# Heads' sums of squares by one fp32 matmul, held operands and another order in the mixer

## The chip, the cores and the metric

The kernel runs on one core of a Trainium2 chip. The metric is the device time of one execution in microseconds, as the median of several runs. Beside the times there is one profiled execution, with every instruction of the five engines: TensorE (PE, its weight loads PEld), VectorE (DVE), ScalarE (ACT), GpSimd (POOL) and SyncE (SP, which issues the DMAs).

## The reference

A decoder trunk of two layers over 512 positions of width 1024. Each layer adds half a SwiGLU feed-forward, a mixer, and half a second feed-forward, each on the RMS-normed stream. Layer 0 mixes by a gated linear recurrence, layer 1 by stick-breaking attention with 16 heads of 64, whose keys and values come from the stream after layer 0. Keys and queries are normed per head:

```python
def shared_kv(x, kv_gain, w_kv, k_gain):
    hkv = rms_norm(x, kv_gain)
    k, v = jnp.split(hkv @ w_kv, 2, axis=-1)
    k = rms_norm(heads(k), k_gain)
    return k, heads(v)

xc = causal_depthwise_conv(rec, conv_w, conv_b)          # rec, gate: h @ w_in
r = sigmoid(block_diag_linear(xc, w_r, b_r)); i = sigmoid(block_diag_linear(xc, w_i, b_i))
a = exp(-8 * r * softplus(-lam)); u = sqrt(1 - a * a) * i * xc
h_t = a_t * h_{t-1} + u_t;   out = (h * gelu(gate)) @ w_out
```

## The kernel before

Activations lie transposed, 128 features by 512 positions to a tile. Every product is made in three matmuls: operand and weight are each split in a high part of type fp32r (a cast) and a low part (what is left, also fp32r), and high x high, low x high and high x low are summed in PSUM. `Weights.split` (L81) does it for weights of 128x1024 (w_hi by ScalarE or GpSimd, w_lo by VectorE), three buffers of each going round. `mm` (L200) issues a matmul. Outside the blocks under `tc.manual_schedule`, a scheduler that works from priorities and modelled durations orders each engine's instructions; the engines then run them strictly in that order, with semaphores for what they need of each other.

The stages, by start in the trace: first feed-forward of layer 0 (0 us), its mixer (356), second feed-forward (519), keys and values (866), first feed-forward of layer 1 (971), attention with its queries (1313), second feed-forward (1528).

**The mixer** walks `RG_ORDER` (L44): "rec" m is a tile of the recurrent branch (24 matmuls), "gate" m one of the gate branch (24), "ri" b the two gates r and i of a block of two tiles (24 matmuls, on the split outputs xc of `conv` (L557) of tiles 2b and 2b+1). What follows a step is queued one to three steps later: conv after its rec, `lru_1` to `lru_3` after an ri, `gate_1` and `gate_2` after a gate. The numbers in the names w_hi102 and so on are places in the plan of weights, 102 being the eleventh entry of the order.

**Keys.** For each of eight pairs of heads there are 24 matmuls into k, then `head_norm` (L668): kx is k over the layer's norm (VectorE), t its square (ScalarE). For all keys and all queries but the first, GpSimd casts t to a high part and VectorE takes the low part (L675, L676), and two fp32r matmuls with `blk`, a block matrix of ones, sum the squares of each head into hs. For query 0 (`qt` given) one matmul takes t and blk as fp32 (L681). Then ScalarE makes y, the inverse root, in three passes, VectorE corrects and multiplies in three (L689 to L691), and the result is split (kh, kl) and stored to DRAM. `head_norm` is a generator in three parts; the caller runs a part of the pair before between the products.

**Values.** Two groups g of four psum tiles, four chunks c each, 24 matmuls to a chunk; hkv is the stationary operand. `v_out` splits and stores them.

**The next feed-forward's operands.** `normed` (L330) makes from two tiles of the stream the seven combinations of its quarter blocks that `pair` (L368) multiplies by seven sums of weight blocks (a form of 24 matmuls over 256 columns each): two multiplications by gain and norm (L335), four sums (L344) and three splits (low parts at L342, L346, L348), nine instructions on VectorE. They depend on the norm r3 alone and on x, so the scheduler may put them early. They are called in the values' loop at three places of g = 0 and one of g = 1 (L767). The first matmuls of the feed-forward need all four.

Of the kernel before, what the change touches and what calls it, by code (L numbers as in the profile page):

```python
# [7 lines left out]
F32 = mybir.dt.float32  # L8
# [32 lines left out]

RG_ORDER = [("rec", 0), ("rec", 1), ("rec", 2), ("rec", 3), ("ri", 0), ("gate", 0), ("ri", 1), ("rec", 4), ("rec", 5), ("gate", 1), ("ri", 2),  # L44
            ("rec", 6), ("rec", 7), ("gate", 2), ("gate", 3), ("ri", 3), ("gate", 4), ("gate", 5), ("gate", 6), ("gate", 7)]

# [101 lines left out]
def trunk(ctx, tc, a, out):  # L150
# [47 lines left out]
        cur.tp = open_pool("tp")  # L198

    def mm(o, l, r, start, stop):  # L200
        nc.tensor.matmul(o, l, r, start=start, stop=stop, skip_group_check=True)  # L201


    prm = cp.tile([P, NPRM], F32, name="prm")
# [122 lines left out]
        nc.vector.tensor_tensor(out=lo, in0=xt, in1=hi.bitcast(F32), op=ALU.subtract)  # L327
        return hi, lo

    def normed(j, g, r, name):  # L330

        e = cur.ep.tile([P, 8, HS], F32, tag="e", name=f"e{name}{j}")
        for k in range(2):
            xt = x[2 * j + k].rearrange("p (c t) -> p c t", c=2)
            nc.vector.scalar_tensor_tensor(out=e[:, 2 * k:2 * k + 2], in0=xt, scalar=gain(g, 2 * j + k), in1=r.rearrange("p (c t) -> p c t", c=2), op0=ALU.mult, op1=ALU.mult)  # L335
        hi = cur.ht.tile([P, 7, HS], F32R, tag="hh", name=f"hh{name}{j}")
        lo = cur.ht.tile([P, 7, HS], F32R, tag="hl", name=f"hl{name}{j}")
        b11, b12, b21, b22 = (e[:, k] for k in range(4))
# [329 lines left out]
    def head_norm(ps, r, g, name, dst, tags, qt=None):  # L668

        kx, t = temp("sq", "kx" + name), temp("acc", "t" + name)  # L670
        nc.vector.tensor_tensor(out=kx, in0=ps, in1=r, op=ALU.mult)
        nc.scalar.activation(out=t, in_=kx, func=AF.Square)
        if qt is None:
            hi, lo = (spare(*tags[j], n + name) for j, n in ((0, "th"), (1, "tl")))
            nc.gpsimd.tensor_scalar(out=hi, in0=t, scalar1=1.0, scalar2=0.0, op0=ALU.mult, op1=ALU.add)  # L675
            nc.vector.tensor_tensor(out=lo, in0=t, in1=hi.bitcast(F32), op=ALU.subtract)  # L676
        yield
        ss = psum("hs" + name)
        y = temp("y", "y" + name, bufs=1)
        if qt is not None:  # L680
            mm(ss, blk.bitcast(F32), t, True, True)  # L681
        else:
            mm(ss, blk, hi, True, False)
            mm(ss, blk, lo, False, True)
        nc.scalar.activation(out=y, in_=ss, func=AF.Ln, scale=1.0 / HD, bias=epsc)
        nc.scalar.activation(out=y, in_=y, func=AF.Exp, scale=-0.5)
        nc.scalar.activation(out=t, in_=y, func=AF.Square)
        yield
        nc.vector.scalar_tensor_tensor(out=t, in0=ss, scalar=HD * EPS, in1=t, op0=ALU.add, op1=ALU.mult)  # L689
        nc.vector.scalar_tensor_tensor(out=y, in0=t, scalar=-3.0 * HD, in1=y, op0=ALU.add, op1=ALU.mult)  # L690
        nc.vector.scalar_tensor_tensor(out=y, in0=kx, scalar=g, in1=y, op0=ALU.mult, op1=ALU.mult)  # L691
        if qt is not None:

            halves = [slice(e * HD, (e + 1) * HD) for e in range(2)]
            for e in range(2):
                nc.gpsimd.tensor_scalar(out=qt[halves[e], 0, e], in0=y[halves[e]], scalar1=1.0, scalar2=0.0, op0=ALU.mult, op1=ALU.add)
                nc.scalar.copy(out=qt[halves[1 - e], 0, e], in_=y[halves[e]])
            for e in range(2):
                for d in (e, 1 - e):
                    nc.vector.tensor_tensor(out=qt[halves[d], 1, e], in0=y[halves[e]], in1=qt[halves[e], 0, e].bitcast(F32), op=ALU.subtract)  # L700
            return
        hi, lo = (spare(*tags[j], n + name) for j, n in ((2, "kh"), (3, "kl")))
        nc.gpsimd.tensor_scalar(out=hi, in0=y, scalar1=1.0, scalar2=0.0, op0=ALU.mult, op1=ALU.add)
        nc.vector.tensor_tensor(out=lo, in0=y, in1=hi.bitcast(F32), op=ALU.subtract)
        for j, t in enumerate((hi, lo)):
            nc.sync.dma_start(dst[j], t.bitcast(F32))
# [7 lines left out]
    for p in range(NPAIR):  # L714
# [15 lines left out]
            nc.vector.scalar_tensor_tensor(out=rc, in0=rt, scalar=-3.0 * D, in1=rc, op0=ALU.add, op1=ALU.mult)  # L730
            nc.vector.tensor_scalar(out=rc, in0=rc, scalar1=-0.5 / D, scalar2=None, op0=ALU.mult)
        kd.append(dp.tile([2, P, S], F32, tag="kd", name=f"kd{p}"))
        gen = head_norm(ps, r3, kg, f"k{p}", kd[p], ((cur.tp, "t3"), (cur.tp, "t4"), (cur.tp, "rec"), (cur.tp, "rec")))
        run(gen)
        run(pend)
        pend = gen
# [12 lines left out]
    for g in range(2):  # L749
        pv = [psum(f"v{g}{s}") for s in range(NCH)]  # L750
        pvs.append(pv)
        if g == 1:
            close_pools(2)
            more_weights()
        for c in range(4):
            hi, lo = W.get(("v", g, c))
            for s in range(NCH):
                ss = slice(s * P, (s + 1) * P)
                for k in range(2):
                    xh, xl = hkv[2 * c + k]  # L760
                    ks = slice(k * S, (k + 1) * S)
                    mm(pv[s], xh[:, ss], hi[:, ks], c == 0 and k == 0, False)
                    mm(pv[s], xh[:, ss], lo[:, ks], False, False)
                    mm(pv[s], xl[:, ss], hi[:, ks], False, c == 3 and k == 1)
            if g == 0 and c < 2:
                run(pend)
            if g == 0 and c > 0 or g == 1 and c == 1:  # L767
                h3.append(normed(len(h3), G_FFN1[1], r3, "n3"))
            if g == 1 and c == 0:
                v_out(0, pvs[0])  # L770

# [136 lines left out]
    def query(p):  # L908

        ps = psum(f"q{p}")  # L910
        if p == 0:
            qts[p] = xp.tile([P, 2, 2, S], F32R, tag="x", name=f"qp{p}")
        return steps(ps, W.get(("q", p)), h4), lambda: head_norm(ps, r4, qg, f"q{p}", qd[p], ((cur.hp, "ch"),) * 4, qts.get(p))


    early = []
# [159 lines left out]
```

## Time and profile before

| | us |
|---|---|
| median of 3 runs (lowest to highest) | 1880.0 (1879.5 to 1881.9) |
| the profiled execution | 1879.0 |
| its span, first to last instruction | 1877.3 |
| keys and values, 865.7 to 970.9 | 105.2 |
| attention with its queries, 1312.9 to 1527.5 | 214.6 |

The span is counted from the first instruction; the profiled execution's own time is 1.7 us more. A row by time gives start, length, engine, line, operation, tiles and shapes, and in brackets the idle time ahead of it with what ended it. A row by line gives busy time and mean length in ns, then the idle time ahead of such instructions. Names stand without their numbers there (hsk is hs of any key pair). Ends of TensorE's rows are modelled; its starts are measured.

### The profile page before, as it was taken

The numbers are of one execution on the slowest core, as the hardware profiler recorded it, in microseconds if no ns is written. First come the engines' busy times: TensorE is split into PE (matmuls) and PEld (weight loads), VectorE is DVE, ScalarE is ACT, GpSimd is POOL, SyncE is SP. The second block draws the span as 40 slices with busy tenths as digits, with TensorE's granted clock in tenths as the row PEclk, the third lists the DMA queues.
The fourth block names the chain that finished last, engine by engine and source line by source line (L and its number), as shares of the span: only waits on it lengthen the run. The fifth ranks groups of instructions, "written<-read, shape, count | busy, mean of one in ns | idle before, by whom it ended". The sixth has DMA issues, their size and how long they took to land.

```text
span 1877.3 us, 27297 instructions
## 1 busy us (share of the span) xinstructions
PE 1839.0 (98%) x11040; PEld 1633.1 (87%) x11040; DVE 1382.4 (74%) x1709; ACT 921.7 (49%) x1282; POOL 156.6 (8%) x196
## 2 busy tenths in 40 slices
PE   9999999999999999999899999999898999999999
PEld 7889989778789899997689899898676789899897
DVE  8958657698788586576978667585799879667483
ACT  6525435368555254354545335254588745345251
POOL 1000000032000000000200000000365500000000
PEclk9999999999999999999999999999999999999999
DMA  6223423222415134232474324134365431425131
GB/s 225 91 79 98 139 71 98 79 79 82 154 46 179 46 101 124 90 93 76 135 213 126 111 79 146 56 111 148 117 188 154 147 92 46 146 79 157 57 109 61
DMA packets 73118, 207.87 MB, mean 111 GB/s; under 512 B 7584, under 2 KB 17056, under 8 KB 72480
## 3 DMA queue, kind: packets, MB, share of 16 engines
q1 hardware_dynamic: 72704, 205.81, 35.3%
q8 instruction: 86, 1.41, 0.3%
q10 hardware_dynamic: 288, 0.32, 0.1%
q14 instruction: 40, 0.33, 0.1%
HBM read 189.85 MB, written 16.25 MB: 110 GB/s over the span
## 4 chain that ended last, share of the span: by engine, by line
PE 44%; DVE 5%; issue 3%; POOL 2%; ACT 1%; SPq 0%; DMA 0%; POOLq 0%; DVEq 0%; ACTq 0%
PE pdffn L201 13%; PE pXffn L201 12%; PE pYffn L201 6%; PE pZffn L201 3%; PE v L201 2%; PE wo L201 2%; PE k L201 2%; PE puffn L201 1%; PE pgffn L201 1%; DVE spl L862 1%; PE z L201 1%; DVE t L862 1%; DVE sp L852 1%; POOL sph L859 0%; DVE w_lo L89 0%
## 5 line engine op out<-in xcount | busy, mean ns | idle before, releaser
L85 ACT CAST w_hi<-w_raw 128x1024 fp32r<-128x1024 f32 (+1 forms) x165 | 165.7, 1007 | 256.5 <-PE pdffn L201 82.5
L85 ACT CAST w_hi<-w_s 128x1024 fp32r<-128x1024 f32 x148 | 155.2, 1050 | 254.0 <-PE pdffn L201 105.4
L89 DVE TENSOR_TENSOR w_lo<-w_raw,w_hi 128x1024 fp32r<-128x1024 f32 (+3 forms) x191 | 219.9, 1154 | 76.8 <-ACT w_hi L85 68.2
L201 PE MATMUL pXffn<-hhffn,w_hi 128*128 128x256 f32 x832 | 235.5, 283 | 0.3 <-ACT effn L389 0.3
L201 PE MATMUL pXffn<-hlffn,w_hi 128*128 128x256 f32 x832 | 235.5, 283 | 0.0
L201 PE MATMUL pXffn<-hhffn,w_lo 128*128 128x256 f32 x832 | 235.5, 283 | 0.0
L201 PE MATMUL pdffn<-ahffn,w_hi 128*128 128x512 f32 x592 | 230.8, 390 | 0.3
L201 PE MATMUL pdffn<-alffn,w_hi 128*128 128x512 f32 x592 | 230.7, 390 | 0.0
L201 PE MATMUL pdffn<-ahffn,w_lo 128*128 128x512 f32 x592 | 230.4, 389 | 0.0
L89 DVE TENSOR_TENSOR w_lo<-w_s,w_hi 128x1024 fp32r<-128x1024 f32 x148 | 180.8, 1221 | 33.1 <-ACT w_hi L85 33.0
L85 ACT CAST w_hi<-w_a 128x1024 fp32r<-128x1024 f32 x111 | 116.5, 1050 | 171.4 <-PE pdffn L201 70.2
L89 DVE TENSOR_TENSOR w_lo<-w_a,w_hi 128x1024 fp32r<-128x1024 f32 x111 | 135.5, 1222 | 36.2 <-ACT w_hi L85 34.8
L201 PEld LDWEIGHTS pXffn<-hhffn,w_hi 128*128 128x128 f32 x832 | 159.7, 192 | 0.8 <-ACT effn L389 0.5
L201 PEld LDWEIGHTS pXffn<-hlffn,w_hi 128*128 128x128 f32 x832 | 159.7, 192 | 0.3
L201 PEld LDWEIGHTS pXffn<-hhffn,w_lo 128*128 128x128 f32 x832 | 159.7, 192 | 0.0
L453 DVE SCALAR_TENSOR_TENSOR x<-pdffn,x 128x512 f32<-128x512 f32 x72 | 49.8, 691 | 141.2 <-PE pdffn L201 141.2
L201 PEld LDWEIGHTS pdffn<-ahffn,w_hi 128*128 128x128 f32 x592 | 111.2, 188 | 24.6 <-ACT ahffn L409 1.8
L201 PEld LDWEIGHTS pdffn<-alffn,w_hi 128*128 128x128 f32 x592 | 111.2, 188 | 24.4 <-DVE alffn L410 1.1
L201 PEld LDWEIGHTS pdffn<-ahffn,w_lo 128*128 128x128 f32 x592 | 111.2, 188 | 22.7
L201 PE MATMUL pYffn<-hhffn,w_hi 128*128 128x256 f32 x416 | 117.7, 283 | 0.0
L201 PE MATMUL pYffn<-hlffn,w_hi 128*128 128x256 f32 x416 | 117.7, 283 | 0.0
L201 PE MATMUL pYffn<-hhffn,w_lo 128*128 128x256 f32 x416 | 117.7, 283 | 0.0
(1154 smaller groups left out, 4691.7 us busy)
## 6 DMA issues: line engine op xcount, KB each, us to landing
w_a<-in_ffn_s SPq DMA_DIRECT2D x148, 512.0 KB, 3.7
w_raw<-in_ffn_w SPq DMA_DIRECT2D x90, 512.0 KB, 4.5
w_raw<-in_ffn_w SPq DMA_DIRECT2D x32, 384.0 KB, 3.4
w_raw<-in_w_in SPq DMA_DIRECT2D x16, 512.0 KB, 3.6
qp<-qd SPq DMA_DIRECT2D x14, 512.0 KB, 5.5
w_raw<-in_w_out SPq DMA_DIRECT2D x8, 512.0 KB, 3.8
w_raw<-in_w_k SPq DMA_DIRECT2D x8, 512.0 KB, 3.6
w_raw<-in_w_v SPq DMA_DIRECT2D x8, 512.0 KB, 3.7
```

The lines of the kernel that those rows point to most:

```text
L85: nc.scalar.copy(out=hi[:, cs], in_=raw[:, cs])
L89: eng.tensor_tensor(out=lo[:, cs], in0=raw[:, cs], in1=hi[:, cs].bitcast(F32), op=ALU.subtract)
L201: nc.tensor.matmul(o, l, r, start=start, stop=stop, skip_group_check=True)
L453: nc.vector.scalar_tensor_tensor(out=x[m], in0=pd, scalar=0.5, in1=x[m], op0=ALU.mult, op1=ALU.add)
L852: nc.vector.scalar_tensor_tensor(out=self.sp, in0=self.z, scalar=0.0, in1=ee, op0=ALU.max, op1=ALU.add)
L862: nc.vector.tensor_tensor(out=lo, in0=src, in1=hi.bitcast(F32), op=ALU.subtract)
```

## The change

Three things. `head_norm` sums t itself for every head, by one matmul of fp32 operands; cast and subtraction are gone, and kh and kl take the tiles t3 and t4, which they had used, in place of "rec" for both. `normed` takes an instruction that its multiplications must not come before in the scheduler's order (a dependence without a semaphore), the last matmul of the values' chunk before it; the fourth is called one chunk sooner. In `RG_ORDER` gate 2 stands ahead of ri 2 instead of behind rec 7.

```diff
-RG_ORDER = [... ("gate", 1), ("ri", 2),
-            ("rec", 6), ("rec", 7), ("gate", 2), ("gate", 3), ("ri", 3), ...]
+RG_ORDER = [... ("gate", 1), ("gate", 2),
+            ("ri", 2), ("rec", 6), ("rec", 7), ("gate", 3), ("ri", 3), ...]
@@ mm
-        nc.tensor.matmul(o, l, r, start=start, stop=stop, skip_group_check=True)
+        return nc.tensor.matmul(o, l, r, start=start, stop=stop, skip_group_check=True)
@@ normed
-    def normed(j, g, r, name):
+    def normed(j, g, r, name, behind=None):
...
-            nc.vector.scalar_tensor_tensor(out=e[:, 2 * k:2 * k + 2], in0=xt, ...)
+            i = nc.vector.scalar_tensor_tensor(out=e[:, 2 * k:2 * k + 2], in0=xt, ...)
+            if behind:
+                tc.add_manual_dep(i.ins, behind.ins.name, NOSYNC, reason="not before other work")
@@ head_norm
-        if qt is None:
-            hi, lo = (spare(*tags[j], n + name) for j, n in ((0, "th"), (1, "tl")))
-            nc.gpsimd.tensor_scalar(out=hi, in0=t, scalar1=1.0, scalar2=0.0, op0=ALU.mult, op1=ALU.add)
-            nc.vector.tensor_tensor(out=lo, in0=t, in1=hi.bitcast(F32), op=ALU.subtract)
...
-        if qt is not None:
-            mm(ss, blk.bitcast(F32), t, True, True)
-        else:
-            mm(ss, blk, hi, True, False)
-            mm(ss, blk, lo, False, True)
+        mm(ss, blk.bitcast(F32), t, True, True)
...
-        hi, lo = (spare(*tags[j], n + name) for j, n in ((2, "kh"), (3, "kl")))
+        hi, lo = (spare(*tags[j], n + name) for j, n in ((0, "kh"), (1, "kl")))
@@ keys, values, queries
-        gen = head_norm(ps, r3, kg, f"k{p}", kd[p], ((cur.tp, "t3"), (cur.tp, "t4"), (cur.tp, "rec"), (cur.tp, "rec")))
+        gen = head_norm(ps, r3, kg, f"k{p}", kd[p], ((cur.tp, "t3"), (cur.tp, "t4")))
...
-                    mm(pv[s], xl[:, ss], hi[:, ks], False, c == 3 and k == 1)
+                    last = mm(pv[s], xl[:, ss], hi[:, ks], False, c == 3 and k == 1)
...
-            if g == 0 and c > 0 or g == 1 and c == 1:
-                h3.append(normed(len(h3), G_FFN1[1], r3, "n3"))
+            if g == 0 and c > 0 or g == 1 and c == 0:
+                h3.append(normed(len(h3), G_FFN1[1], r3, "n3", last))
```

The first place: VectorE among the keys, between kx of pair 4 and kx of pair 5 (en, hl: of `normed`; tk, yk, kl: of `head_norm`; the rows of now have the lines of the changed file). Before, behind kxk4:

```order
L704 TENSOR_TENSOR klk2_8162<-yk2_8143,khk2_8161 128x512
L346 TENSOR_TENSOR hln31_8520<-en31_8516,hhn31_8519 128x1024
L676 TENSOR_TENSOR tlk4_8211<-tk4_8207,thk4_8210 128x512
L348 SCALAR_TENSOR_TENSOR hln31_8520<-en31_8516,hhn31_8519 128x256
L89 TENSOR_TENSOR w_lo223_8282<-w_raw223_8280,w_hi223_8281 128x1024
L689 SCALAR_TENSOR_TENSOR tk3_8151<-hsk3_8198,tk3_8151 128x512
L335 SCALAR_TENSOR_TENSOR en32_8561<-x1_79,prm_75,rs_n3_7968 128x512
L690 SCALAR_TENSOR_TENSOR yk3_8199<-tk3_8151,yk3_8199 128x512
L335 SCALAR_TENSOR_TENSOR en32_8561<-x1_79,prm_75,rs_n3_7968 128x512
L691 SCALAR_TENSOR_TENSOR yk3_8199<-kxk3_8150,kg_1004,yk3_8199 128x512
L344 TENSOR_TENSOR en32_8561<-en32_8561 128x256
L671 TENSOR_TENSOR kxk5_8262<-k5_8223,rs_n3_7968 128x512
```

Now:

```order
L673 TENSOR_TENSOR kxk4_8186<-k4_8148,rs_n3_7968 128x512
L89 TENSOR_TENSOR w_lo222_8202<-w_raw222_8200,w_hi222_8201 128x1024
L683 SCALAR_TENSOR_TENSOR tk3_8136<-hsk3_8179,tk3_8136 128x512
L684 SCALAR_TENSOR_TENSOR yk3_8180<-tk3_8136,yk3_8180 128x512
L685 SCALAR_TENSOR_TENSOR yk3_8180<-kxk3_8135,kg_1004,yk3_8180 128x512
L698 TENSOR_TENSOR klk3_8194<-yk3_8180,khk3_8193 128x512
L673 TENSOR_TENSOR kxk5_8237<-k5_8199,rs_n3_7968 128x512
```

The six rows of `normed` and the subtraction tlk4 have left; klk3 is through ahead of kxk5. All four normed now follow klk7, between the values' weight subtractions.

The second place: VectorE in the mixer, from the low part of weight 103 (rec 6 before, ri 2 now) to that of conv 5. Before, behind w_lo103:

```order
L564 SCALAR_TENSOR_TENSOR xc4_3802<-rect4_3799,prm_75,xc4_3802 128x512
L560 TENSOR_TENSOR rect5_3854<-rec5_3823,rs_n1_3453 128x512
L610 SCALAR_TENSOR_TENSOR s_2_3811<-g0_2_3752,s_2_3811 128x512
L327 TENSOR_TENSOR xc4l_3808<-xc4_3802,xc4h_3807 128x512
L564 SCALAR_TENSOR_TENSOR xc5_3857<-rect5_3854,prm_75,xc5_3857 128x512
L611 TENSOR_TENSOR g1_2_3754<-g1_2_3754,s_2_3811 128x512
L564 SCALAR_TENSOR_TENSOR xc5_3857<-rect5_3854,prm_75,xc5_3857 128x512
L613 SCALAR_TENSOR_TENSOR hs2_3868<-a0_2_3762,g1_2_3754 128x512
L564 SCALAR_TENSOR_TENSOR xc5_3857<-rect5_3854,prm_75,xc5_3857 128x512
L610 SCALAR_TENSOR_TENSOR s_3_3816<-g0_3_3756,s_3_3816 128x512
L89 TENSOR_TENSOR w_lo104_3901<-w_raw104_3899,w_hi104_3900 128x1024
L327 TENSOR_TENSOR xc5l_3863<-xc5_3857,xc5h_3862 128x512
```

Now:

```order
L89 TENSOR_TENSOR w_lo103_3850<-w_raw103_3848,w_hi103_3849 128x1024
L327 TENSOR_TENSOR xc4l_3808<-xc4_3802,xc4h_3807 128x512
L566 SCALAR_TENSOR_TENSOR xc5_3857<-rect5_3854,prm_75,xc5_3857 128x512
L612 SCALAR_TENSOR_TENSOR s_2_3811<-g0_2_3752,s_2_3811 128x512
L566 SCALAR_TENSOR_TENSOR xc5_3857<-rect5_3854,prm_75,xc5_3857 128x512
L613 TENSOR_TENSOR g1_2_3754<-g1_2_3754,s_2_3811 128x512
L566 SCALAR_TENSOR_TENSOR xc5_3857<-rect5_3854,prm_75,xc5_3857 128x512
L615 SCALAR_TENSOR_TENSOR hs2_3868<-a0_2_3762,g1_2_3754 128x512
L612 SCALAR_TENSOR_TENSOR s_3_3816<-g0_3_3756,s_3_3816 128x512
L327 TENSOR_TENSOR xc5l_3863<-xc5_3857,xc5h_3862 128x512
```

The last steps of conv 4 and the division of rec 5 (rect5) moved ahead of w_lo103, whose cast went from GpSimd to ScalarE; hs2 and s_3 stand behind conv 5's last step, and w_lo104 behind xc5l.

The third place: TensorE at ("ri", 2). Before:

```order
L201 MATMUL gate1_3874<-n1a7h_3407,w_lo101_3735 128x512
L201 MATMUL ri40_3908<-xc4h_3807,w_hi102_3794 128x512
L201 MATMUL ri41_3915<-xc4h_3807,w_hi102_3794 128x512
L201 MATMUL ri50_3922<-xc4h_3807,w_hi102_3794 128x512
L201 MATMUL ri40_3908<-xc4l_3808,w_hi102_3794 128x512
L201 MATMUL ri40_3908<-xc4h_3807,w_lo102_3795 128x512
L201 MATMUL ri41_3915<-xc4l_3808,w_hi102_3794 128x512
L201 MATMUL ri41_3915<-xc4h_3807,w_lo102_3795 128x512
L201 MATMUL ri50_3922<-xc4l_3808,w_hi102_3794 128x512
L201 MATMUL ri50_3922<-xc4h_3807,w_lo102_3795 128x512
L201 MATMUL ri51_3929<-xc4h_3807,w_hi102_3794 128x512
```

Now:

```order
L201 MATMUL gate2_3908<-n1a7h_3407,w_lo102_3795 128x512
L201 MATMUL ri40_3947<-xc4h_3807,w_hi103_3849 128x512
L201 MATMUL ri40_3947<-xc4l_3808,w_hi103_3849 128x512
L201 MATMUL ri40_3947<-xc4h_3807,w_lo103_3850 128x512
L201 MATMUL ri40_3947<-xc5h_3862,w_hi103_3849 128x512
L201 MATMUL ri40_3947<-xc5l_3863,w_hi103_3849 128x512
L201 MATMUL ri40_3947<-xc5h_3862,w_lo103_3850 128x512
L201 MATMUL ri41_3954<-xc4h_3807,w_hi103_3849 128x512
```

All of gate 2 now stands ahead; behind it the first psum tile takes its three xc4 matmuls and then xc5's, where twelve xc4 matmuls and eight of rec 6 came before the first of xc5.

## Rows read from the trace of the kernel before

**Rows 1.** The page, part 1: busy us (share of the span) xinstructions.

```profile
PE 1839.0 (98%) x11040; PEld 1633.1 (87%) x11040; DVE 1382.4 (74%) x1709; ACT 921.7 (49%) x1282; POOL 156.6 (8%) x196
```

**Rows 2.** TensorE by time, keys to feed-forward: start, length, line, out<-in, [idle before].

```profile
865.67 0.39 PE L201 MATMUL k<-n3a0h,w_hi 128*128 128x512 f32 x1
...
870.66 1.02 PE L297 MATMUL ss_n<-acc_n,onesf 128*128 128x512 f32 x2
871.11 0.79 PE L201 MATMUL k<-n3a7l,w_hi 128*128 128x512 f32 x1
871.74 0.39 PE L201 MATMUL k<-n3a7h,w_lo 128*128 128x512 f32 x1
...
877.91 0.39 PE L201 MATMUL k<-n3a7l,w_hi 128*128 128x512 f32 x1
878.14 0.39 PE L201 MATMUL k<-n3a7h,w_lo 128*128 128x512 f32 x1
881.17 0.80 PE L201 MATMUL hsk<-thk,blk 128*128 128x512 f32 x1 [2.65 <-POOL thk L675]
...
883.04 0.63 PE L201 MATMUL hsk<-tlk,blk 128*128 128x512 f32 x1
...
970.90 0.28 PE L201 MATMUL pXffn<-hhn,w_hi 128*128 128x256 f32 x1
```

**Rows 3.** Busy us by stage; after POOL: granted clock, DMA share, GB/s.

```profile
412.50:435.10 22.60, 18.25 (x74) 14.34 (x73) 17.57 (x22) 12.77 (x16) 5.69 (x7) 0.92 0.28 84
865.70:931.00 65.30, 58.10 (x240) 45.99 (x239) 56.15 (x89) 33.73 (x54) 10.60 (x12) 0.95 0.37 118
931.00:970.90 39.90, 39.28 (x173) 32.20 (x172) 30.50 (x38) 19.09 (x26) 3.42 (x4) 1.00 0.67 213
1342.00:1485.00 143.00, 128.65 (x641) 100.77 (x640) 135.92 (x205) 114.84 (x238) 89.94 (x115) 0.96 0.57 155
```

**Rows 4.** TensorE in order of time around ("ri", 2) in the mixer.

```profile
412.34 0.39 PE L201 MATMUL gate<-n1a7h,w_lo 128*128 128x512 f32 x1
416.64 1.55 PE L201 MATMUL ri<-xc4h,w_hi 128*128 128x512 f32 x3 [3.91 <-ACT xc4h L326]
...
434.89 0.39 PE L201 MATMUL rec<-n1a7h,w_lo 128*128 128x512 f32 x1
```

**Rows 5.** ScalarE and GpSimd in order of time, ahead of the first heads' sum.

```profile
879.29 1.15 ACT L672 ACTIVATE tk<-kxk 128x512 f32<-128x512 f32 x2
...
879.99 1.70 POOL L675 TENSOR_SCALAR thk<-tk 128x512 fp32r<-128x512 f32 x2 [410.34 <-ACT tk L672]
```

**Rows 6.** VectorE from 873.5 to 925.8 by line; then one instruction by time.

```profile
L344 DVE TENSOR_TENSOR en<-en 128x256 f32<-128x256 f32 x12 | 5.2, 450 | 0.0
L676 DVE TENSOR_TENSOR tlk<-tk,thk 128x512 fp32r<-128x512 f32 x7 | 5.1, 745 | 2.6 <-POOL thk L675 2.6
...
L335 DVE SCALAR_TENSOR_TENSOR en<-x,prm,rs_n 128x512 f32<-128x512 f32 x6 | 4.4, 742 | 0.0
...
L346 DVE TENSOR_TENSOR hln<-en,hhn 128x1024 fp32r<-128x1024 f32 x3 | 3.7, 1223 | 0.0
...
L342 DVE TENSOR_TENSOR hln<-en,hhn 128x512 fp32r<-128x512 f32 x3 | 2.0, 681 | 0.0
L348 DVE SCALAR_TENSOR_TENSOR hln<-en,hhn 128x256 fp32r<-128x256 f32 x3 | 1.3, 419 | 0.0
...
889.51 0.69 DVE L704 TENSOR_TENSOR klk<-yk,khk 128x512 fp32r<-128x512 f32 x1
```

**Rows 7.** VectorE in order of time, same place.

```profile
411.54 1.53 DVE L602 SCALAR_TENSOR_TENSOR s<-s,a 128x512 f32<-128x512 f32 x1
...
413.65 1.62 DVE L89 TENSOR_TENSOR w_lo<-w_raw,w_hi 128x1024 fp32r<-128x1024 f32 x1
...
423.94 0.68 DVE L327 TENSOR_TENSOR xc5l<-xc,xc5h 128x512 fp32r<-128x512 f32 x1
```

**Rows 8.** VectorE in attention, by line and shape.

```profile
L676 DVE TENSOR_TENSOR tlq<-tq,thq 128x512 fp32r<-128x512 f32 x6 | 5.5, 921 | 1.8 <-POOL thq L675 1.8
```

More of the change, by code (lines that the diff above doesn't have):

```diff
@@ L40 @@
 C_CONVW, C_CONVB, C_BR, C_BI, C_LAM, C_KG, C_QG, NPRM = 56, 88, 96, 104, 112, 120, 121, 122
-RG_ORDER = [("rec", 0), ("rec", 1), ("rec", 2), ("rec", 3), ("ri", 0), ("gate", 0), ("ri", 1), ("rec", 4), ("rec", 5), ("gate", 1), ("ri", 2),
-            ("rec", 6), ("rec", 7), ("gate", 2), ("gate", 3), ("ri", 3), ("gate", 4), ("gate", 5), ("gate", 6), ("gate", 7)]
+RG_ORDER = [("rec", 0), ("rec", 1), ("rec", 2), ("rec", 3), ("ri", 0), ("gate", 0), ("ri", 1), ("rec", 4), ("rec", 5), ("gate", 1), ("gate", 2),
+            ("ri", 2), ("rec", 6), ("rec", 7), ("gate", 3), ("ri", 3), ("gate", 4), ("gate", 5), ("gate", 6), ("gate", 7)]
 class Weights:
@@ L334, in normed @@
             xt = x[2 * j + k].rearrange("p (c t) -> p c t", c=2)
-            nc.vector.scalar_tensor_tensor(out=e[:, 2 * k:2 * k + 2], in0=xt, scalar=gain(g, 2 * j + k), in1=r.rearrange("p (c t) -> p c t", c=2), op0=ALU.mult, op1=ALU.mult)
+            i = nc.vector.scalar_tensor_tensor(out=e[:, 2 * k:2 * k + 2], in0=xt, scalar=gain(g, 2 * j + k), in1=r.rearrange("p (c t) -> p c t", c=2), op0=ALU.mult, op1=ALU.mult)
+            if behind:
+                tc.add_manual_dep(i.ins, behind.ins.name, NOSYNC, reason="not before other work")
         hi = cur.ht.tile([P, 7, HS], F32R, tag="hh", name=f"hh{name}{j}")
@@ L912, in query @@
             qts[p] = xp.tile([P, 2, 2, S], F32R, tag="x", name=f"qp{p}")
-        return steps(ps, W.get(("q", p)), h4), lambda: head_norm(ps, r4, qg, f"q{p}", qd[p], ((cur.hp, "ch"),) * 4, qts.get(p))
+        return steps(ps, W.get(("q", p)), h4), lambda: head_norm(ps, r4, qg, f"q{p}", qd[p], ((cur.hp, "ch"),) * 2, qts.get(p))
     early = []
```

## Prediction

> **What bounds the kernel now.** I read the page's busy shares first, then the busy time by stage, then the instructions in order of time on TensorE and on the engine that ended each of its waits. The page has TensorE busy for 98% of the span [rows 1], which would leave nothing to gain. But those ends are modelled: a matmul row of 512 columns says 0.39 us while the next one starts 0.227 us later (877.91, 878.14) [rows 2]. So I count TensorE's need as matmuls times 0.227 us and call the rest of a stretch its stall.
>
> Three stretches that the change touches have much stall. **Keys and values**, from the first key matmul (865.67) to the first of the next feed-forward (970.90), take 105.2 us [rows 2]. Their need: 8 x 24 key matmuls, 16 for the heads' sums and 192 for the values, 400 x 0.227 = 90.8, and 1.7 for the two sums of the layer norm (0.85 each, below): 92.5. Stall 12.7, all but 1 of it among the keys, where VectorE is busy for 56 of 65 us [rows 3]. **The mixer around ("ri", 2)**: from the end of gate 1 (412.57) to that of rec 7 (435.12) 72 matmuls need 16.3 of 22.55 us: 6.2 of stall, 4.1 of it ahead of the first ri matmul [rows 4]. **Attention**: VectorE is busy for 135.9 of 143 us, TensorE's weight loads for 100.8 [rows 3]; VectorE sets the pace there.
>
> The Trainium skill says the same of the measure (Perfetto Trace Analysis, Identifying the Most-Contended Engine): matmul busy time misleads since matmuls are pipelined, and weight-load busy time should be read instead. The page's 98% would put 6 us on this kernel for the longer sums (last rival), its rule leaves room for a gain; the starts in the trace [rows 2] side with the rule.
>
> **The change, part by part.**
>
> *One fp32 matmul for two.* The norm's sum has the form that the change uses, an fp32 matmul over 512 columns. From its start at 870.66 to the key matmul at 871.74 lie it (two records) and one other matmul [rows 2]: 1.08 - 0.227 = 0.85 us. The two matmuls that it replaces take 0.454, so each sum costs 0.40 more: 8 keys 3.2 us, 7 queries 2.8 (query 0 has it already). Gone are, for each of these 15 heads, a GpSimd cast and a VectorE subtraction; no DMA comes or goes, only the order of SP's changes.
>
> *Keys.* Two things make a sum late. One is the split: the first sum starts at 881.17, 2.8 us after the keys of head pair 1 end, released by GpSimd's cast, which had begun at 879.99, when the square stood [rows 2, 5]. The square alone lets it start at about 880.0: 1.5 us of wait instead of 2.8. The other is VectorE's queue: the next layer's operands (27 instructions of `normed` for three of four j, with the subtraction `tlk` beside them) stand between one head's chain and the next, as the first place in the order shows; by the rows of the group that is 2 x 0.74 + 4 x 0.45 + 0.68 + 1.22 + 0.42 = 5.6 us for each normed and 0.75 for each tlk [rows 6]. The change takes both out. What is left for a pair is some 5 us of VectorE work in 24 x 0.227 + 0.85 = 6.3 us of TensorE, with the square ready a product ahead. So all key stalls but the first go. The granted clock of 0.95 over the 65.3 us [rows 3] says that 6.5 us ran at 1.2 GHz instead of 2.4, behind the two waits of 2.8 us; with a wait of 1.5 I take it to stay up (if not, 1.6 us are lost, as long as the slow rows lasted).
>
> New length: 384 x 0.227 + 8 x 0.85 + 1.7 + 1.5 = 97.2 us. The feed-forward could start at 962.9 instead of 970.9: a gain of 8.0.
>
> *Operands held.* The edge is of order only, no semaphore. The four normed now follow `klk7` on VectorE. That instruction: the last sum ends after 216 matmuls, 8 sums, 1.7 and 1.5, at 924.7, and the first head's low part `klk0` was written 6.7 us after its sum (from 883.5 to 890.2) [rows 2, 6]: 931.4. From there VectorE has to get through 4 x 5.6, seven weight subtractions and three weight sums (1.22 each, as L346's shape), and six of the values' at 0.74: 22.4 + 12.2 + 4.5 = 39.1, or 36 when the 0.08 by which starts in a full queue come before ends is taken off 40 times. That ends at 967.5 to 970.5. Due is the third form's first low part, 962.9 + 48 x 0.114 + 0.23 = 968.6 (256 columns, so half of 0.227). So between 1.1 of slack and 1.9 of lack; I take 0.5 away. The values' own weights stand in between with over 3 us each. Net for keys and values: **-7.5** (bounds -8.5 and, with the clock lost and the lack in full, -4).
>
> *Mixer.* Gate 2 moves ahead of ("ri", 2), whose first matmul then starts at 412.6 + 5.4 = 418.0. It needs conv 4 and conv 5. In the new order (the second place) `xc5l` has eight instructions between it and w_lo103 where eleven stood, and the weight cast for slot 103 leaves GpSimd, beside which s_3 took 1.53 and w_lo 1.62 [rows 7] instead of 0.69 and 1.22. I get w_lo103 at 414.1 and `xc5l`, which was written at 424.6, at 422.3. But on TensorE (the third place) xc5 stands behind only three xc4 matmuls: stall 422.3 - 418.0 - 0.9 = 3.4. That is 2.8 less than 6.2; I keep 0.8 back for a clock that may fall there as it does now (0.92 granted over this stretch [rows 3]). The later ("ri", 3) now has one gate less ahead of it; by the same count its xc7 comes within 1 us of its need, as now. **-2.0** (bounds +1 if that wait grows, -4.5 if conv 5 is in time).
>
> *Attention.* Six `tlq` of 0.92 go, 5.5 us, and the first one's 1.8 of waiting for GpSimd [rows 8], of which I count 1.1, since the next head's rows wait for ScalarE anyway. Without the cast on GpSimd other subtractions run at the keys' 0.75 rather than 0.92: 6 x 0.2 = 1.2. Together 7.8 off an engine that is 95% busy. TensorE pays 7 x 0.40; a third of that I put on the path, and of the relief nearly a fifth is lost to other engines' waits: **-5.5** (bounds -1.5 and -9; nearest is the row with VectorE at 95%).
>
> The Trainium skill goes further (SBUF — State Buffer, Who interferes with whom): a VectorE instruction with two SBUF inputs and a GpSimd one that reads SBUF exclude each other, and the second waits in full. By it each cast could cost a subtraction its whole 0.6 us, 3.7 us for six, and the time would come out 2 lower; the rows show 0.2 to 0.9 a piece [rows 7, 8], so the sum stays with them.
>
> **Sum.** 7.5 + 2.0 + 5.5 = 15.0. The profiled execution took 1879.0 us (span 1877.3, 1.7 around it); 1879.0 - 15.0 = 1864.0. The median of the runs, 1880.0, is 1.0 above the profiled one: **1865**.
>
> **The rivals.** *A. Attention's relief is not passed on.* TensorE, GpSimd and ScalarE wait for each other in turn there, and the added 2.8 us of TensorE falls between. Then 1.5 instead of 5.5: 1869. Against it: VectorE's 5% of idle time.
> *B. The operands come late.* VectorE's queue from 931 to 969 has no room, as counted; a wait for a weight transfer or for a value's store inside it comes straight to the feed-forward's start. At worst 7 of the 7.5 go back: 1872. For it: such waits exist now between 945 and 971 (VectorE is busy for 30.5 of 39.9 us [rows 3]); against it: they came from having nothing else to do.
> *A and B together:* 1876.
> *C. TensorE is the bound, slower.* If the sums' starts hang on the square and not on the split or the queue, all waits stay, and 15 x 0.40 = 6 us are added: 1886. This decides at the key that follows a normed: if its division by the norm (kxk) still starts after the next product's end. The order shows nothing left ahead of it but a weight's subtraction, and the first wait shows 1.3 of 2.8 us from the split, so I give it little.
>
> **How the numbers follow.** A measurement of this kernel can tell about 0.2%, 3.8 us. Forecast 0.60 (1858 to 1868), A 0.15, B 0.15, both 0.06, C 0.04. Faster by over 0.2%: 0.90; within: 0.06; slower: 0.04. The range takes the good bounds (8.5 + 4.5 + 9 = 22 less, 1858, and one for the run) and reaches over A and B: 1857 to 1873.
>
> **What would show it.** Right: the keys' sums start within 0.3 us of the product before, but for the first (near 1.5); the feed-forward's first matmul comes 7 to 8 us earlier against the first key; VectorE is full from there to its start. ("ri", 2) starts at once behind gate 2 and then waits some 3 us for xc5. Attention's 48 units take 5 to 6 us less, VectorE still over 90% busy. Wrong: a wait for `w_lo` or `hln3` at the feed-forward's start (B), attention as long as before with VectorE's share fallen (A), or sums that wait for the square (C).

## The result and the profile after

The changed kernel takes 1869.9 us (median of 6 runs, 1868.9 to 1870.5) against 1880.3 us before (6 runs, 1879.5 to 1881.9): a ratio of 0.9943, with an interval of 0.993 to 0.9956. It is faster by 10.4 us; 15 had been forecast. The profiled execution took 1870.0 us with a span of 1868.2, against 1879.0 and 1877.3, so the trace accounts for 9.1 of it.

A unit of attention is the work on one of six blocks of a pair of heads, 48 in all (z are its scores, O its output). The lengths below run from the first matmul of a stage to the first of the next, read from TensorE in order of time in each trace. A stage that is missing differs by less than 0.1; the first varies from 355.3 to 358.3 between kernels that are alike in it.

| stage | before | after | difference | forecast |
|---|---|---|---|---|
| first feed-forward | 356.1 | 356.4 | +0.3 | 0 |
| mixer with output projection | 163.0 | 163.7 | +0.7 | -2.0 |
| keys and values | 105.2 | 97.8 | -7.5 | -7.5 |
| attention's queries, ahead of the first unit | 21.3 | 21.8 | +0.4 | in the next |
| attention's units and its projection | 193.3 | 190.3 | -3.0 | -5.5 |
| sum | | | -9.1 | -15.0 |

The page has TensorE busy for 98% of the span, as before [rows 1]; VectorE has 15 instructions less, GpSimd too:

```profile
PE 1837.1 (98%) x11040; PEld 1627.9 (87%) x11040; DVE 1369.8 (73%) x1694; ACT 921.4 (49%) x1282; POOL 141.6 (8%) x181
```

**Keys.** TensorE in order of time, as in [rows 2]: the first key matmul, the wait ahead of the first sum, a later sum, and the feed-forward's first matmul.

```profile
866.66 0.39 PE L201 MATMUL k<-n3a0h,w_hi 128*128 128x512 f32 x1
...
879.13 0.39 PE L201 MATMUL k<-n3a7h,w_lo 128*128 128x512 f32 x1
880.96 1.12 PE L201 MATMUL hsk<-tk,blk 128*128 128x512 f32 x2 [1.44 <-ACT tk L674]
...
887.18 0.39 PE L201 MATMUL k<-n3a7h,w_lo 128*128 128x512 f32 x1
887.40 1.02 PE L201 MATMUL hsk<-tk,blk 128*128 128x512 f32 x2
887.86 0.79 PE L201 MATMUL k<-n3a0h,w_hi 128*128 128x512 f32 x1
888.49 0.39 PE L201 MATMUL k<-n3a0l,w_hi 128*128 128x512 f32 x1
...
964.42 0.28 PE L201 MATMUL pXffn<-hhn,w_hi 128*128 128x256 f32 x1
```

The first sum waits 1.60 us behind the last product's step (879.13 + 0.227 to 880.96) instead of 2.8, and ScalarE's square ends it. All later sums are on time, as the one at 887.40, 0.22 behind the product ahead of it. From that start to 888.49 there is one other matmul: 1.09 - 0.227 = 0.86 us for a sum. The busy time by stage, at the places of [rows 3] (mixer, keys, values, and attention's units for 143 us and to their end):

```profile
412.80:435.40 22.60, 18.93 (x72) 14.83 (x71) 19.38 (x24) 12.05 (x16) 5.95 (x6) 0.85 0.34 101
866.66:931.99 65.33, 63.89 (x268) 49.46 (x267) 44.76 (x63) 33.39 (x52) 4.98 (x8) 1.00 0.44 144
931.99:964.42 32.43, 32.43 (x144) 26.84 (x143) 32.30 (x51) 17.97 (x25) 0.00 (x0) 1.00 0.58 176
1328.18:1471.18 143.00, 126.87 (x640) 97.87 (x638) 131.17 (x198) 114.56 (x239) 84.90 (x107) 0.99 0.54 151
1328.18:1518.48 190.30, 173.85 (x846) 135.48 (x844) 161.41 (x237) 137.92 (x275) 91.50 (x116) 0.99 0.52 150
```

The mixer's granted clock fell from 0.92 to 0.85, that of the keys rose from 0.95 to 1.00, of attention (143 us as in [rows 3]) to 0.99 from 0.96. VectorE, among the values, is busy for 32.3 of 32.4 us. There the held operands stand, VectorE in order of time:

```profile
931.65 0.69 DVE L698 TENSOR_TENSOR klk<-yk,khk 128x512 fp32r<-128x512 f32 x1 [0.80 <-POOL khk L697]
932.26 1.41 DVE L335 SCALAR_TENSOR_TENSOR en<-x,prm,rs_n 128x512 f32<-128x512 f32 x2
...
957.96 1.22 DVE L348 TENSOR_TENSOR hln<-en,hhn 128x1024 fp32r<-128x1024 f32 x1
```

`klk7` starts at 931.65 and the first multiplication of `normed` follows it at once, but the last low part, `hln3`, starts at 957.96. It was due some 5.7 us behind the feed-forward's start, at 970.1: 10.9 us of slack, where I had counted between 1.1 of slack and 1.9 of lack.

**Mixer.** TensorE around ("ri", 2), to be held against [rows 4]:

```profile
418.08 0.39 PE L201 MATMUL gate<-n1a7h,w_lo 128*128 128x512 f32 x1
418.31 0.39 PE L201 MATMUL ri<-xc4h,w_hi 128*128 128x512 f32 x1
...
418.76 0.39 PE L201 MATMUL ri<-xc4h,w_lo 128*128 128x512 f32 x1
420.86 0.51 PE L201 MATMUL ri<-xc5h,w_hi 128*128 128x512 f32 x1 [1.72 <-ACT xc5h L326]
423.32 0.80 PE L201 MATMUL ri<-xc5l,w_hi 128*128 128x512 f32 x1 [1.96 <-DVE xc5l L327]
...
428.61 0.40 PE L201 MATMUL ri<-xc5l,w_hi 128*128 128x512 f32 x1
...
441.36 0.39 PE L201 MATMUL gate<-n1a0h,w_hi 128*128 128x512 f32 x1
```

and VectorE, which writes the low part of xc5, then GpSimd at the same time:

```profile
416.10 1.53 DVE L566 SCALAR_TENSOR_TENSOR xc<-rect,prm,xc 128x512 f32<-128x512 f32 x1
...
421.21 1.46 DVE L612 SCALAR_TENSOR_TENSOR s<-g,s 128x512 f32<-128x512 f32 x1
422.59 0.68 DVE L327 TENSOR_TENSOR xc5l<-xc,xc5h 128x512 fp32r<-128x512 f32 x1
```

```profile
414.69 2.41 POOL L87 TENSOR_SCALAR w_hi<-w_raw 128x1024 fp32r<-128x1024 f32 x1
...
420.41 1.73 POOL L87 TENSOR_SCALAR w_hi<-w_raw 128x1024 fp32r<-128x1024 f32 x1
```

("ri", 2) follows gate 2 at once, as forecast, and then stops twice, 1.9 us for the high part of xc5 and 2.2 for its low part. Ahead of each stop it did what was ready: three matmuls, then one. The matmuls behind come 0.43 apart instead of 0.227 until 428.6; from 423.32 to there that costs 2.6 us. So from the end of gate 2 to that of rec 7 (418.31 to 441.36) the 72 matmuls take 23.05 us, of which 6.7 are stall, where it was 6.2 of 22.55 before. Behind it, up to the output projection, hardly anything changed: 0.7 us of stall before, 0.5 now.

### The profile page after: what moved, and what is told of

It reads as the page before. It is cut to its first block, busy times and chain, and to the rows that moved or that the text cites. A ratio compares the mean times of both kernels' runs of the same rounds, so it can differ in the third digit from the quotient of the medians.

```text
span 1868.2 us, 27263 instructions
## 1 busy us (share of the span) xinstructions
PE 1837.1 (98%) x11040; PEld 1627.9 (87%) x11040; DVE 1369.8 (73%) x1694; ACT 921.4 (49%) x1282; POOL 141.6 (8%) x181
```

## The experiments

Each edit is against the changed kernel, each time the median of the runs beside 1879.9 to 1880.9 us for the kernel before. Lengths of stages come from the profiled execution of each.

**The old order of the mixer** alone put back.

```diff
-("gate", 1), ("gate", 2), ("ri", 2), ("rec", 6), ("rec", 7), ("gate", 3), ("ri", 3)
+("gate", 1), ("ri", 2), ("rec", 6), ("rec", 7), ("gate", 2), ("gate", 3), ("ri", 3)
```

> The changed kernel with the mixer's old order (gate 2 behind rec 7). Theory: the new order is worth nothing, or a little less than nothing (from the first rec to the first wout matmul 118.2 us with it, 117.8 without); this kernel then comes out 0 to 1 us under the changed one's 1869.9, near 1869.3, and that stretch at 117.8. Rival: the new order gains the 2.0 that were forecast and the loss came from elsewhere; then about 1872 and a stretch near 120.

1869.7 us (0.994, 0.9925 to 0.9955). The old wait is back, TensorE in order of time:

```profile
411.55 0.39 PE L201 MATMUL gate<-n1a7h,w_lo 128*128 128x512 f32 x1
415.86 1.65 PE L201 MATMUL ri<-xc4h,w_hi 128*128 128x512 f32 x3 [3.93 <-ACT xc4h L326]
```

The mixer with its projection takes 163.7, exactly as with the new order (118.5 and 45.2). Eight executions of kernels with the new order lie between 162.6 and 163.8 there, and what parts them is the granted clock over this stretch: 163.7 and 163.8 at 0.98, 162.6 to 162.8 in the six at 0.99. With the old order it is 163.7 at 0.98 (this run) and 163.0 at 0.99 (the kernel before). At the same clock the two orders lie within 0.4 of each other, and the first theory stands, but for its 117.8 (118.5 measured).

**Rec 6 ahead of ri 2 as well.**

```diff
-("gate", 2), ("ri", 2), ("rec", 6), ("rec", 7), ("gate", 3), ("ri", 3)
+("gate", 2), ("rec", 6), ("ri", 2), ("rec", 7), ("gate", 3), ("ri", 3)
```

> The changed kernel with rec 6 ahead of ri 2 as well: 5.4 us more of products in front of the first matmul that needs conv 4 and conv 5. Theory: VectorE's queue fixes when conv 5 is written (423.3 us), whatever TensorE does; ri 2 then starts at 423.8 and its two waits (1.9 and 2.2) and the half clock behind them (2.8) are gone: 4 to 6.5 us less, 1863.5 to 1866. Rival: conv 6 and conv 7 come later by as much and the wait moves to ri 3: 0 to 2 us less, 1868 to 1870.

1870.9 us (0.9949, 0.9934 to 0.9964): the rival. TensorE around the two, in order of time:

```profile
424.23 0.39 PE L201 MATMUL ri<-xc5h,w_hi 128*128 128x512 f32 x1
424.45 0.39 PE L201 MATMUL ri<-xc5l,w_hi 128*128 128x512 f32 x1
...
441.23 0.39 PE L201 MATMUL ri<-xc6h,w_hi 128*128 128x512 f32 x1
447.75 1.22 PE L201 MATMUL ri<-xc7h,w_hi 128*128 128x512 f32 x2 [6.13 <-ACT xc7h L326]
```

("ri", 2) runs without a stop, and ("ri", 3) now waits 6.3 us behind its last step for xc7. The mixer and the projection take 164.4.

**Gate 4 ahead of ri 3 too.**

```diff
-("gate", 2), ("ri", 2), ("rec", 6), ("rec", 7), ("gate", 3), ("ri", 3), ("gate", 4)
+("gate", 2), ("rec", 6), ("ri", 2), ("rec", 7), ("gate", 3), ("gate", 4), ("ri", 3)
```

> The changed kernel with rec 6 ahead of ri 2 and gate 4 ahead of ri 3 as well: 5.4 us more of products in front of each of the two, the same work in all. Theory: VectorE's queue fixes when conv 5 and conv 7 are written; with the earlier order ri 2 had no wait left and ri 3 waited 6.3 us for conv 7, so 5.4 more covers most of it and the clock behind it: from the first rec to the feed-forward 5 to 7 us less than the changed kernel's 163.6, near 1864. Rival: with one gate less behind ri 3 its scan and the last y come late and the output projection waits as long: 0 to 2 less, 1868 to 1870.

1870.5 us (0.9947, 0.9932 to 0.9962), mixer and projection 164.0: the rival again. Part of the wait has gone from ("ri", 3), which still stops twice, on to the output projection, which waits 4.1 us for y5, an output of the mixer that it multiplies:

```profile
447.89 0.50 PE L201 MATMUL ri<-xc7h,w_hi 128*128 128x512 f32 x1 [1.60 <-ACT xc7h L326]
449.99 0.51 PE L201 MATMUL ri<-xc7l,w_hi 128*128 128x512 f32 x1 [1.60 <-DVE xc7l L327]
...
479.16 0.79 PE L201 MATMUL wout<-y5h,w_hi 128*128 128x512 f32 x1 [4.08 <-ACT y5h L326]
```

Four orders put the wait in four places (ahead of ("ri", 2), within it, at ("ri", 3), and at ("ri", 3) and the projection), and the stretch takes 162.6 to 164.4 in all of them. What the rows name at the end of each wait is a conv's output or a y, written by ScalarE or VectorE; the order of TensorE's products only says where it waits for them.

**The held operands** put back among the keys.

```diff
-            if g == 0 and c > 0 or g == 1 and c == 0:
-                h3.append(normed(len(h3), G_FFN1[1], r3, "n3", last))
+            if g == 0 and c > 0 or g == 1 and c == 1:
+                h3.append(normed(len(h3), G_FFN1[1], r3, "n3"))
```

> The changed kernel without the held operands: three of four normed among the keys again, sums still by one fp32 matmul. Theory: the queue of VectorE carries most of the keys' gain, so the sums behind a normed start late again; from the first key matmul to the feed-forward's first 97.8 us become 102 to 104, the time about 1875. Rival: the split carried most, the queue little; then 98 to 99.5 and about 1871.

1870.5 us (0.9949, 0.9933 to 0.9966). Keys and values take 99.5 us, at the upper end of the rival's range: without the split, VectorE gets through the operands and the heads' chains alike. Only the first and the seventh of the eight sums wait, 1.4 and 1.5 us idle for the square:

```profile
880.16 1.12 PE L201 MATMUL hsk<-tk,blk 128*128 128x512 f32 x2 [1.44 <-ACT tk L674]
...
919.95 1.12 PE L201 MATMUL hsk<-tk,blk 128*128 128x512 f32 x2 [1.47 <-ACT tk L674]
```

**The two matmuls of cast and rest** put back, operands still held (the tiles of kh and kl as before too, not shown).

```diff
         nc.scalar.activation(out=t, in_=kx, func=AF.Square)
+        if qt is None:
+            hi, lo = (spare(*tags[j], n + name) for j, n in ((0, "th"), (1, "tl")))
+            nc.gpsimd.tensor_scalar(out=hi, in0=t, scalar1=1.0, scalar2=0.0, op0=ALU.mult, op1=ALU.add)
+            nc.vector.tensor_tensor(out=lo, in0=t, in1=hi.bitcast(F32), op=ALU.subtract)
...
-        mm(ss, blk.bitcast(F32), t, True, True)
+        if qt is not None:
+            mm(ss, blk.bitcast(F32), t, True, True)
+        else:
+            mm(ss, blk, hi, True, False)
+            mm(ss, blk, lo, False, True)
```

> The changed kernel with the sums by two matmuls of a cast and a rest again (keys and queries), operands still held, gate 2 still ahead. Theory: in the keys the hold alone does nearly all; the sums cost 3.2 us less of TensorE, but the first waits 1.2 us longer and may cost 1.6 of clock: keys and values 96.5 to 98.5; attention falls back by 2.6, so about 1872.5. Rival: without the shorter chain every key's sum is late by 0.5 to 1 us: keys and values 101 to 104 and about 1877.

1873.4 us (0.9964, 0.995 to 0.9977). Keys and values take 99.3 us, 0.8 above the theory's range and far under the rival's. TensorE in order of time: the first sum, and two waits that are new, in the next feed-forward:

```profile
881.33 0.79 PE L201 MATMUL hsk<-thk,blk 128*128 128x512 f32 x1 [2.65 <-POOL thk L677]
...
971.77 0.39 PE L201 MATMUL pXffn<-hhn,w_hi 128*128 128x256 f32 x1 [0.78 <-ACT effn L391]
...
984.74 0.39 PE L201 MATMUL pXffn<-hhn,w_hi 128*128 128x256 f32 x1 [1.18 <-DVE effn L399]
```

The first sum waits 2.8 us for GpSimd's cast as in the kernel before, and the busy time by stage shows the clock that goes with it, down until 887:

```profile
870.83:887.00 16.17, 13.52 (x50) 10.40 (x49) 8.52 (x15) 7.18 (x13) 1.70 (x2) 0.80 0.30 96
887.00:926.00 39.00, 39.00 (x171) 31.69 (x169) 29.60 (x41) 20.24 (x30) 8.28 (x12) 0.99 0.46 149
```

The other sums are in time. Attention's units take 193.6 us, against 193.3 in the kernel before and 190.3 in the changed one. But the feed-forward behind the keys, 342.0 us in the changed kernel, takes 344.5: two blocks' products find TensorE idle for 0.8 and 1.2 us ahead of them, for `effn`, the tile into which ScalarE and VectorE take the blocks' products out of PSUM. VectorE in order of time, `klk7` and the write of `effn` that ends the second wait:

```profile
935.74 0.69 DVE L706 TENSOR_TENSOR klk<-yk,khk 128x512 fp32r<-128x512 f32 x1 [0.52 <-POOL khk L705]
...
984.00 0.68 DVE L399 TENSOR_TENSOR effn<-pXffn,effn 128x512 f32<-128x512 f32 x1
```

The same write in the changed kernel:

```profile
980.85 0.68 DVE L399 TENSOR_TENSOR effn<-pXffn,effn 128x512 f32<-128x512 f32 x1
```

It starts 47.6 us behind the end of `klk7` here and 48.5 in the changed kernel, and VectorE is idle for 1.6 and 1.7 us of that: the held operands, the values and the weights behind them fill its queue up to this write. But the feed-forward starts 28.7 us behind `klk7` here and 32.1 in the changed kernel, where `effn` stands 0.2 us before it is needed. So the two parts can be set side by side (keys and values, and in brackets with the feed-forward behind them):

| us | operands not held | held |
|---|---|---|
| two matmuls of cast and rest | 105.2 (447.2) | 99.3 (443.8) |
| one fp32 matmul | 99.5 (441.5) | 97.8 (439.8) |

Either part alone removes most of the keys' stall; together they give 7.5, not 5.7 + 6.0. The hold alone loses 2.5 again behind its end, the fp32 sum loses nothing. The medians say the same more coarsely: 1873.4 without the fp32 sum (in keys and queries), 1870.5 without the hold and 1869.9 with both, so that what the hold adds to the fp32 sum can't be told from nothing there.

**Sums of rounded squares**, keys and queries: ScalarE writes the square as fp32r into a tile of its own (one more at the calls, not shown), one fp32r matmul adds it up, and the rounding's rest is left out.

```diff
-        nc.scalar.activation(out=t, in_=kx, func=AF.Square)
+        hi = t if qt is not None else spare(*tags[2], "th" + name)
+        nc.scalar.activation(out=hi, in_=kx, func=AF.Square)
...
-        mm(ss, blk.bitcast(F32), t, True, True)
+        mm(ss, blk if qt is None else blk.bitcast(F32), hi, True, True)
```

> The changed kernel with ScalarE writing the squares rounded to fp32r and one fp32r matmul for each sum (15 of 16; query 0 stays): no cast, no subtraction, and 0.23 instead of 0.86 us of TensorE. It leaves out the rounding's rest, so the sums differ in their last bits. Theory: TensorE's longer sums are on the path in full, in the keys and in attention: 8 x 0.63 = 5.0 and 7 x 0.63 = 4.4 come back, about 1860.5. Rival: in attention only a third of them counts, as forecast: 5.0 + 1.5, about 1863.5.

1868.3 us (0.9935, 0.9921 to 0.995): both theories miss. TensorE among the keys, in order of time:

```profile
885.54 0.40 PE L201 MATMUL hsk<-thk,blk 128*128 128x512 f32 x1
885.78 0.39 PE L201 MATMUL k<-n3a0h,w_hi 128*128 128x512 f32 x1
```

A sum takes 0.24 us, keys and values 92.5: 5.2 less, as both had it. But the feed-forward behind takes 1.5 more, and attention's units 193.2, which is 2.9 more with 3.8 us less of TensorE's work in them, in another order of instructions and at a granted clock of 0.96 instead of 0.99. The same **for the keys alone**:

```diff
-        nc.scalar.activation(out=t, in_=kx, func=AF.Square)
+        hi = spare(*tags[2], "th" + name) if name[0] == "k" else t
+        nc.scalar.activation(out=hi, in_=kx, func=AF.Square)
...
-        mm(ss, blk.bitcast(F32), t, True, True)
+        mm(ss, blk if name[0] == "k" else blk.bitcast(F32), hi, True, True)
```

> The changed kernel with the keys' sums alone by one fp32r matmul of squares that ScalarE writes rounded; queries as in the change. It leaves out the rounding's rest of the keys' sums. Theory: as where keys and queries were both rounded, keys and values 5.2 us shorter (92.5), 1.3 to 1.5 given back to a wait in the feed-forward's first blocks, attention as in the changed kernel (190.3): about 1866. Rival: attention's loss of 2.9 there came from the keys' side (their buffers and transfers), not from the queries' sums; then 1869.

1866.2 us (0.9922, 0.9905 to 0.9938), as the theory has it: keys and values 92.6, attention's units 190.3. So the 2.9 came from the queries' side. Behind the keys 1.5 us are given back, most of it in one wait of TensorE in the feed-forward, which starts 29.5 us behind `klk7` with `effn` again 47.5 behind it:

```profile
978.69 0.39 PE L201 MATMUL pXffn<-hhn,w_hi 128*128 128x256 f32 x1 [1.14 <-DVE effn L399]
```

This version has a lower median than both kernels, though its interval touches the changed kernel's, and it leaves the rest of the squares out. With the edit of gate 4 and rec 6 added (the two diffs together):

> The edits of the two kernels before this one together, the rest of the keys' sums left out as there. Theory: they lie 400 us apart and add: the changed kernel less 4 for the keys and less 5 to 7 for the mixer, 1859 to 1861. Rival: the mixer's part moves the wait only, 1865 to 1866.

1865.8 us (0.9923, 0.9909 to 0.9938), mixer and projection 162.9: the rival, as the four orders say.

**Attention, each engine's work alone.** Queries' sums computed twice, into the same place:

```diff
+        if name[0] == "q" and qt is None:
+            mm(ss, blk.bitcast(F32), t, True, True)
         mm(ss, blk.bitcast(F32), t, True, True)
```

> The changed kernel with the seven queries' sums (all but query 0) computed twice into the same place: 7 x 0.86 = 6.0 us more of TensorE in attention, nothing else. Theory: TensorE's time is on the path there in full: about 1875.9, the 48 units and wo longer by 6. Rival: a third of it, as forecast: 2 longer, about 1871.9.

1872.8 us (0.996, 0.9945 to 0.9975): between the two, nearer the rival. One of the seven sums lies ahead of the units and cost 0.9 there; the other six, 5.2 us, made the units 2.8 longer. One more subtraction on VectorE for each of seven queries:

```diff
+        if name[0] == "q" and qt is None:
+            lo = spare(*tags[1], "tl" + name)
+            nc.vector.tensor_tensor(out=lo, in0=t, in1=kx, op=ALU.subtract)
```

> The changed kernel with one more subtraction of 128 x 512 on VectorE for each of seven queries, right behind the square, its result unused: 7 x 0.75 = 5.3 us more of VectorE in attention, no cast and no matmul. Theory that VectorE sets the pace there: 4 to 5.5 longer, 1874 to 1875.5. Rival that after the change the engines wait for each other in turn and VectorE has slack: 0 to 2 longer, 1870 to 1872.

1871.6 us (0.9953, 0.9937 to 0.997), under the theory's range; the units are 2.2 us longer. And three of them:

```diff
+        if name[0] == "q" and qt is None:
+            for n in range(3):
+                lo = spare(*tags[1], f"tl{n}" + name)
+                nc.vector.tensor_tensor(out=lo, in0=t, in1=kx, op=ALU.subtract)
```

> The changed kernel with three more subtractions of 128 x 512 on VectorE for each of seven queries, results unused: 6 x 3 x 0.75 = 13.5 us more of VectorE within the 48 units. Theory from the run with one (4.5 us of work cost 2.2): half of VectorE's time is on the path, +6.5 to 7, about 1877. Rival: the slack is used up after the first and all further work counts in full: +2.2 and 9, about 1881; or one and three cost about the same since the loss was a lower clock alone: 1872 to 1873.

1875.9 us (0.9976, 0.9967 to 0.9986), near the half. The busy time of attention's units, up to the first matmul behind them, first of the kernel before:

```profile
1334.22:1527.52 193.30, 176.18 (x845) 138.87 (x844) 167.97 (x243) 138.21 (x276) 97.33 (x123) 0.96 0.52 147
```

The same with the sums twice:

```profile
1327.36:1520.48 193.12, 178.07 (x857) 139.33 (x856) 162.78 (x236) 137.36 (x275) 87.96 (x116) 0.98 0.53 147
```

with one more subtraction:

```profile
1327.48:1520.02 192.54, 176.39 (x846) 136.99 (x844) 167.04 (x243) 137.83 (x275) 89.23 (x116) 0.98 0.53 148
```

and with three more:

```profile
1327.36:1522.91 195.55, 178.05 (x845) 137.94 (x844) 172.33 (x255) 138.70 (x275) 92.42 (x116) 0.97 0.52 146
```

Against the changed kernel's 190.30, with VectorE busy for 161.41: one subtraction brings 5.6 us of work and 2.2 of length, three bring 10.9 and 5.3. So 0.4 to 0.5 us of length come with one of VectorE, and 2.8 / 5.2 = 0.54 with one of TensorE. Neither sets the pace alone. These shares are not of the added work alone: each of the three edits also sorted the units' instructions anew and had a granted clock of 0.97 to 0.98 instead of 0.99, and no run parts the three.

## Why the prediction was right, and where it was off

The measured time lies in the range of 1857 to 1873, but above the forecast case's own 1858 to 1868, and only one of the three terms had the right size. By its number it is rival A's 1869, and that is chance: attention gave 2.6, between A's 1.5 and the 5.5 forecast, and the mixer's 2.0 did not come.

**Keys and values** came as worked out: 7.5. The first wait (1.5 forecast, 1.6 measured), the clock that stays up behind it and the sums in time were right. Two small errors cancel: the new length was 97.8 instead of 97.2, and the 0.5 for late operands did not come, since they had 10.9 us of slack. My queue had about the right prices but not the right members: I put seven weight subtractions, three weight sums and six of the values ahead of the last operand, while the scheduler put five, none and three ahead of `hln3`. What I did not see is that the two causes overlap. "The change takes both out" is true, but taking out either was enough for 5.7 or 6.0 of the 7.5. Rival B was a real danger all the same, at another place than the `w_lo` or `hln3` that it named: VectorE's queue has no room up to `effn`, and with the split still there this cost the next feed-forward 2.5.

**Mixer.** "-2.0" was wrong: 0 at the same clock, 0.7 more in this one execution. ("ri", 2) started at once behind gate 2, as told, but the stretch to the end of rec 7 kept its stall: 6.7 us, where I had 3.4 and 0.8 for the clock, and 6.2 before. Two terms were mis-sized. The wait was 4.1 instead of 3.4, since `xc5l`, started at 422.59, was written at 423.3 and not at 422.3. Of that 0.3 is this execution's later start; and two instructions of VectorE ahead of it took 1.53 and 1.46 us where the same kinds take 0.74 and 0.68, both while GpSimd cast a weight: it still cast two weights there. And the clock cost 2.6 instead of 0.8. The step that looked at this wait alone had a second fault. With more products in front of it the wait at ("ri", 2) did go, and came back at ("ri", 3) and at the output projection, in both orders that were tried.

**Attention.** "-5.5" was twice too large: 2.6, its queries' 0.4 more included. VectorE's busy time fell by 6.6 us, from 167.97 to 161.41, of which 5.5 are the six subtractions [rows 8] and 1.1 the others' shorter times; I had 1.2 for those. (By the Trainium skill's rule that I weighed, SBUF — State Buffer, Who interferes with whom, it would have been 3.7.) The term was mis-sized at "of the relief nearly a fifth is lost": the runs give a half, 2.6 to 3.3 us. And "a third of that I put on the path" is 0.54 by the doubled sums: 2.4 us of added matmul in the units cost 1.3. That makes 1.3 to 2.0 less; 3.0 was measured. Rival A was half true, then: VectorE's 95% did not mean that it set the pace. The Trainium skill (Perfetto Trace Analysis, Identifying the Most-Contended Engine) has the engine of the highest occupancy relieved first; here that was worth half of what it was relieved of: VectorE is still busy for 131.2 of 143 us, 92%, and the units are 3.0 shorter for 6.6 us less of its work.

The last 1.0 to 1.7 us are not settled. Each edit of the queries' sums makes the scheduler sort the units' instructions anew, and the rounded sums show that such a new order with less work can be 2.9 longer. The clock is another candidate, and the runs disagree on it. The units of the kernel with the two matmuls put back stand in the same order on TensorE, VectorE, GpSimd and ScalarE as those of the kernel before, and take 193.6 us at a granted clock of 0.98 against 193.3 at 0.96:

```profile
1330.95:1524.52 193.57, 174.99 (x845) 136.38 (x844) 168.40 (x243) 138.15 (x276) 97.11 (x123) 0.98 0.52 147
```

The units of six other runs stand in the same order as the changed kernel's. Four of them take 190.2 to 190.3 at 0.99, as it does, and two take 189.2 and 189.3 at 1.00. One of these, the run without the hold:

```profile
1329.14:1518.42 189.28, 172.27 (x846) 134.26 (x845) 161.90 (x237) 137.64 (x275) 91.22 (x116) 1.00 0.53 151
```

So a clock 0.02 higher went with 0.3 more in the old order, and one 0.01 higher with 1.0 less in the new one.

**Rival C** did not come: only the first sum waits for the square, the others are on time, and with the split put back the first waits 1.2 us longer.

## What to carry to other kernels

A wait that one engine's queue sets is not removed by putting other products in front of it: look for where it comes back before a gain is written down, and price a reorder over the whole stage. Two causes of one stall do not add; try each alone before both are paid for. Where several engines hand work round in a loop, the busiest one's share does not say what a microsecond of it is worth, but a doubled piece of work gives an idea of it, with the new order and clock that come with it: here about half, for two engines at once.

## What the runs showed of the hardware

How a stop and a lower clock go together was less regular than I had taken it. Two stops of 1.9 and 2.2 us with a matmul between them left the mixer's matmuls 0.43 apart until 428.6, five us behind the last; one of 2.8 among the keys did so until 887 (with the two matmuls put back), and one of 1.6 not at all. In attention, of seven executions with the same instructions in the same order, five had such a stretch near the start of the units and two had none; the two are 1.0 us shorter (busy time by stretch, the granted clock behind GpSimd's column). The changed kernel:

```profile
1334.00:1336.00 2.00, 2.00 (x9) 1.81 (x8) 1.02 (x3) 1.60 (x5) 0.00 (x0) 0.50 0.00 0
```

and the run without the hold:

```profile
1334.00:1336.00 2.00, 2.00 (x12) 1.73 (x12) 0.07 (x1) 2.00 (x6) 0.00 (x0) 1.00 0.30 123
```

A granted clock of 0.50 is the 1.2 GHz level. TensorE had stopped for 2.6 us shortly before in both, behind the matmul of 1329.22 in the first and of 1330.18 in the second, and the records don't tell why only one fell.
